# A decoder layer with sparse attention on one NeuronCore: where the rotary embedding's products and sums stand in the attention's queues

## The chip, the core and the metric

The kernel runs on one core of a Trainium2 chip. A core has five engines with a queue each, taken in order: TensorE (PE in the profile, with PEld for its weight loads), VectorE (DVE), ScalarE (ACT), GpSimd (POOL) and SyncE (SP), which here only starts DMAs. The metric is device time in microseconds, the median of several executions. One execution was also recorded by the hardware profiler, and all rows come from it.

## The reference

One layer in float32 over 512 tokens of width 1024, then a final norm:

```
h = rms_norm(x);  proj = h @ w_in          # u, q, kc, vc, ks, vs, kw, vw, g_nsa, g_merge
y_pool = causal pooling mixer of u (windows 2, 4, 8, 16)
y_nsa  = gate0 * softmax(q k_cmp) v_cmp    # 31 compressed blocks of keys
       + gate1 * softmax(q ks) vs          # selected blocks: with 8 blocks and 16 picks, all of them
       + gate2 * softmax(q kw) vw          # sliding window of 512: all causal keys
x += (g_a * (y_pool @ w_proj_pool) + g_b * (y_nsa @ w_proj_nsa)) @ w_out
x += square(relu(rms_norm(x) @ w_ff1)) @ w_ff2
out = rms_norm(x)
```

There are 16 heads of 64 in two groups. q, ks and kw (and the compressed keys) get the rotary embedding, rope: `x * cos + rot(x) * sin`, where rot swaps the two halves of 32 of each head, with a sign.

## The kernel before

Float32 is kept by splitting operands in a high and a low half (fp32r); a product is three matmuls, high by high, high by low, low by high. A weight tile of 1024 columns is loaded to `raw` (L235), copied to a high half on ScalarE (L351) and subtracted to a low half on VectorE or GpSimd (L353).

The first stage (to about 180 us) projects the keys, the values, the first three q and the pooling mixer. The attention stage (about 183 to 388 us) walks over 96 *slots*, 12 for each of the 8 pairs of heads: slots 0 to 3 of a pair are its first half (query blocks 0 and 1, both branches together), slots 4 to 11 its second half, the long ones (blocks 2 and 3, one branch each). After it come the output projection and the MLP (from about 480 us), in a fast matrix product whose sums of weights are made in DRAM by copies (L265, on SP) and accumulating DMAs (L273, on GpSimd), some of them during the attention.

One slot i goes through: scores into a PSUM bank on TensorE (`score_pe`, L1016, three banks); masked negative maximum on VectorE (`smax`, L1038); exponential with its sum on ScalarE (`expo`, L1048); a reciprocal on VectorE (L1058) and the weighting by it and the gate on GpSimd (`weight`, L1061); four slots later the transposition on TensorE (`turn_pe`, L1078, two banks); the high half of the result on ScalarE (`turn_hi`, L1089) and the low half on VectorE (`turn_lo`, L1093), the *PT*; two slots later the product with the values (`pv`, L1112). Once per pair `cmp_scores` does the compressed branch, L952 to L988, whose normaliser times gate, `c` of 128x8, is the small gate product (L973, VectorE), followed by three GpSimd operations (L975, L977, L978); its result opens each accumulation `psO` (L1103), which also needs the sums that empty the bank before (L1121, VectorE).

Between the slots stands *filler*: the projections of q3 to q7 and of the merge gate's second half (`fill2`, L394, 24 matmuls each), advanced so that it is spread over the slots. Each q goes through `rope`: ScalarE evacuates the bank to `rx` (L619), four DMAs on SP write its swapped quarters to `rs` (L622), four products with the cosine and sine tables, half a row each, in place (L631: on VectorE in the first stage, on GpSimd in the attention), two sums on VectorE (L634, L636), and then `q_done` makes Q's high halves on ScalarE (L661, L662) and low halves on VectorE (L664, L666). There is one `rx` and one `rs`, and the next q's projection isn't begun before the rope in hand is done (`scored["rope"]`).

`rope`, `cmp_scores` and others are generators: each `yield` passes on to the other work, and `step_side` steps all that are under way once per slot. In the attention a product of the rope isn't emitted unless the slot before was one of a second half (`slot["long"]`), and it is put behind that slot's weighting (`slot["scaled"]`, through `behind`, which places an instruction after another in issue order). The emission order is not the final one: a scheduler orders each engine's instructions from it, with all dependences kept. q3's rope falls in pair 0, q4's in pair 1, q5's in pair 2, q6's in pair 3 and q7's in pair 5.

Of the kernel before, what the change touches and what calls it, by code (L numbers as in the profile page):

```python
# [13 lines left out]
F32 = mybir.dt.float32  # L14
FR = mybir.dt.float32r
AF = mybir.ActivationFunctionType
ALU = mybir.AluOpType
# [45 lines left out]
def trunk(ctx: ExitStack, tc: tile.TileContext, A, out):  # L63
    nc = tc.nc
    PE, ACT, DVE, POOL = nc.tensor, nc.scalar, nc.vector, nc.gpsimd
    PSUM = bass.MemoryType.PSUM

    def pool(name, **kw):
        return tc.tile_pool(name=name, bufs=1, reuse_waits="tile", **kw)
# [206 lines left out]
    mode = {"pool": False, "first": POOL}  # L276
# [202 lines left out]
    op = e2.enter_context(pool("op"))  # L479
# [8 lines left out]
    GT = ap.tile([128, NT, 48], F32, name="GT")  # L488
# [40 lines left out]
    def behind(made):  # L529
        return tc.issue_after(made.ins)  # L530
# [3 lines left out]
    def sums0(i):  # L534
        junk = p0.tile([128, D], F32, tag="junk", bufs=1, name="junk")
        ACT.activation(junk, xt[i], AF.Square, accum_out=rr[i][:, 0:1])
        r = ACT.activation(rr[i][:, 1:2], rr[i][:, 0:1], AF.Sqrt, bias=eps_t, scale=1.0 / D)
        DVE.reciprocal(rr[i][:, 2:3], rr[i][:, 1:2])
        for h in range(2):
            c = slice(512 * h, 512 * h + 512)  # L540
            v = DVE.scalar_tensor_tensor(xt[i][:, c], xt[i][:, c], rr[i][:, 2:3], psg[h], op0=ALU.mult, op1=ALU.mult)
        return r, v
# [10 lines left out]
    def evac0(i, after=None):  # L553
        sl = slice(128 * i, 128 * i + 128)
        for a in range(2):
            ks = slice(4 * a, 4 * a + 4)
            r = ACT.activation(hT[0][:, ks, sl], trs[i][a], AF.Copy)
            with behind(after) if after else nullcontext():
                v = DVE.tensor_tensor(hT[1][:, ks, sl], trs[i][a], hT[0][:, ks, sl].bitcast(F32), op=ALU.subtract)
        return r, v  # L560
# [9 lines left out]
    r, _ = evac0(1)  # L570
    stir(3)
    with behind(r):
        sums0(2)
        r, v = sums0(3)
# [33 lines left out]

    scored = {"pairs": 0, "rope": 0}
    last_exp = []  # L610
    slot = {"long": False, "scaled": None}

    def rope(ps, scale, done, after=0):

        assert not scored["rope"]
        scored["rope"] = 1
        xr = ap.tile([128, S], F32, tag="rx", bufs=1, name="rx")
        sw = ap.tile([128, S], F32, tag="rs", bufs=1, name="rs")
        ACT.activation(xr, ps, AF.Copy, scale=scale)  # L619
        for b in range(4):  # L620
            a = b ^ 1
            nc.sync.dma_start(sw[32 * b:32 * b + 32, :], xr[32 * a:32 * a + 32, :])  # L622
        yield
        eng = POOL if mode["pool"] else DVE
        hs = [slice(0, S // 2), slice(S // 2, S)]
        for c in hs:
            for t, table in ((xr, cosT), (sw, sinT)):
                while mode["pool"] and not slot["long"]:
                    yield
                with behind(slot["scaled"]) if mode["pool"] else nullcontext():  # L630
                    eng.tensor_tensor(t[:, c], t[:, c], table[:, c], op=ALU.mult)  # L631
                yield
                if c is hs[1] and t is xr:
                    DVE.tensor_tensor(xr[:, hs[0]], xr[:, hs[0]], sw[:, hs[0]], op=ALU.add)  # L634
        yield
        DVE.tensor_tensor(xr[:, hs[1]], xr[:, hs[1]], sw[:, hs[1]], op=ALU.add)  # L636
        while scored["pairs"] < after:
            yield
        for _ in done(xr):
            yield  # L640
        scored["rope"] = 0
# [16 lines left out]
    def q_done(p):  # L658
        def done(q):
            t = ap.tile([128, 2, S], FR, tag="Q", bufs=3, name="Q")  # L660
            ACT.activation(t[0:64, 0, :], q[0:64, :], AF.Copy)  # L661
            ACT.activation(t[64:128, 1, :], q[64:128, :], AF.Copy)  # L662
            yield
            DVE.tensor_tensor(t[64:128, 0, :], q[0:64, :], t[0:64, 0, :].bitcast(F32), op=ALU.subtract)  # L664
            yield
            DVE.tensor_tensor(t[0:64, 1, :], q[64:128, :], t[64:128, 1, :].bitcast(F32), op=ALU.subtract)  # L666
            Q[p] = t
        return done
# [223 lines left out]
    with ExitStack() as c2:  # L892
# [54 lines left out]
        def cmp_scores(p):  # L947
            g = p // 4
            ps = ps2.tile([128, NT, 2, 64], F32, tag="S", bufs=S_BANKS, name="psC")
            for qb in range(NT):  # L950
                for h in range(2):
                    PE.matmul(ps[:, qb, h, :], Q[p][:, h, 128 * qb:128 * qb + 128], KC[g], start=True, stop=True,  # L952
                              skip_group_check=True)
            w = p2.tile([128, NT, 2, 64], F32, tag="cw", bufs=1, name="cw")
            s8 = p2.tile([128, 3, 8], F32, tag="c8", bufs=1, name="c8")
            cm = cst[:, C_CM:C_CM + 128].rearrange("p (q n) -> p q n", q=NT)
            wl = w[:, :, :, 0:32]
            wf = w.rearrange("p q h n -> p (q h) n")[:, :, 0:32]
            DVE.tensor_tensor(wl, ps[:, :, :, 0:32], cm[:, :, None, :].to_broadcast([128, NT, 2, 32]), op=ALU.add)
            sc = ps.rearrange("p q h n -> p (q h) n")[:, :, 0:32]  # L960
            DVE.tensor_tensor(ps[:, :, :, 0:32], ps[:, :, :, 32:64], wl, op=ALU.add)
            yield
            DVE.tensor_reduce(s8[:, 0, :], sc, axis=AX.X, op=ALU.min)
            DVE.tensor_tensor(wf, sc, s8[:, 0, :, None].to_broadcast([128, 8, 32]), op=ALU.subtract)
            yield
            yield
            yield
            ACT.activation(wl, wl, AF.Exp, scale=-1.0)
            yield
            DVE.tensor_reduce(s8[:, 1, :], wf, axis=AX.X, op=ALU.add)  # L970
            DVE.reciprocal(s8[:, 2, :], s8[:, 1, :])
            r = s8[:, 2, :].rearrange("p (q h) -> p q h", q=NT)
            DVE.tensor_tensor(r, r, GT[:, :, 6 * p:6 * p + 6:3], op=ALU.mult)  # L973
            yield
            POOL.tensor_tensor(wl, wl, r[:, :, :, None].to_broadcast([128, NT, 2, 32]), op=ALU.mult)  # L975
            pH, pL = (PC[:, :, e, :].rearrange("p q (h n) -> p q h n", h=2) for e in range(2))
            POOL.tensor_scalar(pH, wl, 1.0, 1.0, op0=ALU.mult, op1=ALU.mult)  # L977
            POOL.tensor_tensor(pL, wl, pH.bitcast(F32), op=ALU.subtract)  # L978
            yield
            yield  # L980
            yield
            yield
            pt = ps2.tile([128, S], F32, tag="T", bufs=T_BANKS, name="psT")
            for qb in range(NT):
                src = PC[:, qb, :, :].rearrange("p e c -> p (e c)")
                PE.transpose(pt[:, 128 * qb:128 * qb + 128].bitcast(FR), src, identR)
            t = p2.tile([128, S], FR, tag="pc", bufs=1, name="pc")
            ACT.activation(t, pt, AF.Copy)  # L988
            PTc[p] = t
# [100 lines left out]

        def turn_lo(i):
            src, dH, dL = turn_views(i)
            DVE.tensor_tensor(dL, src, dH.bitcast(F32), op=ALU.subtract)  # L1093
            live.pop(i)

        def pv(i):
            p, half, br, qb, h = slots[i]
# [37 lines left out]
        for i in range(n + LAG + PLAG):  # L1135
            if i < n:
                p = slots[i][0]
                if i % 12 == 3 and p + 1 < NPAIR:
                    while p + 1 not in Q:
                        fill()  # L1140
                        step_side()
                if i % 12 == CMP_AT and p + 1 < NPAIR:
                    side.append(cmp_scores(p + 1))
            if i + 1 < n:
                score_pe(i + 1)
                scored["pairs"] = (i + 2) // 12
            t = i - LAG
            if 0 <= t < n:
                turn_pe(t)
                turn_hi(t)  # L1150
            if i < n:
                smax(i)
                expo(i)
            if 0 <= i - 1 < n:
                last = weight(i - 1)
                slot.update(long=i > 3 and slots[i - 1][1] == 1, scaled=last)
            if i > 7 and i % 4 == 3 and len(begun) > 1:
                add_sum(last)
            if 0 <= t < n:
                turn_lo(t)  # L1160
            step_side()
            want = done0 + (total - done0) * (i + 1) // (n + LAG + PLAG)
            while fdone[0] < want and fill():
                pass
            if i < 5:
                fill()
            j = t - PLAG
            if 0 <= j < n and j % 2 == 1 and pv(j):
                o_evac(*slots[j][0:2])
# [492 lines left out]
```

## Time and profile before

| what | value |
|---|---|
| median of 3 runs | 811.16 us (810.91 to 811.49) |
| the profiled execution | 812.4 us |
| its span, first to last instruction | 810.6 us |
| mean granted TensorE clock | 0.995 |
| TensorE busy | 786.0 us, 97% |
| VectorE busy | 621.0 us, 77% |
| ScalarE busy | 491.3 us, 61% |
| GpSimd busy | 188.8 us, 23% |

A row of an operation gives the line, the engine, the operation, output and inputs, and a count; after the bar busy time, mean duration, and idle time before it with what ended it. In the chronological rows the first number is the start in us, the second the duration, and brackets hold the idle time of the engine just before and its releaser.

### The profile page before, as it was taken

How to read it: one execution, taken by the hardware profiler on the slowest of the kernel's cores; microseconds unless marked ns; L12 is line 12 of the kernel's file. 1: busy time of each engine (PE TensorE's matmuls, PEld its weight loads, DVE VectorE, ACT ScalarE, POOL GpSimd, SP SyncE). 2: the span in 40 equal slices, each digit the busy share in tenths (PEclk: the TensorE clock that was granted, in tenths of full speed). 3: DMA queues.
4: the chain of work that ended last, by engine and by line, in shares of the span. 5: the costliest groups of instructions: out<-in, count | busy, mean ns of one | idle time of the engine just before them, and what ended most of it. 6: DMA issues, size and time to landing. Idle time of an engine off the chain costs nothing.

```text
span 810.6 us, 14129 instructions
## 1 busy us (share of the span) xinstructions
PE 786.0 (97%) x5163; PEld 708.2 (87%) x5163; DVE 621.0 (77%) x1231; ACT 491.3 (61%) x968; POOL 188.8 (23%) x259
## 2 busy tenths in 40 slices
PE   8999999999799999899999999999999999999996
PEld 6889878888677888788888899999999999999996
DVE  5786744539888888789555579996889688978975
ACT  6666533329777888799534476844674467447833
POOL 4000000028676867666010100111010110000000
PEclk9999999999999999999999999999999999999999
DMA  9464632353587524353975706999998998654522
GB/s 294 139 175 109 178 92 89 107 156 92 98 188 153 104 71 96 77 108 74 310 207 181 184 1 190 324 232 292 255 279 220 288 258 230 192 177 156 181 80 105
DMA packets 128751, 136.65 MB, mean 169 GB/s; under 512 B 5349, under 2 KB 117001, under 8 KB 128522
## 3 DMA queue, kind: packets, MB, share of 16 engines
q1 hardware_dynamic: 107274, 113.98, 43.5%
q0 software_dynamic: 21120, 20.97, 18.1%
q8 instruction: 41, 0.67, 0.3%
q10 hardware_dynamic: 288, 0.79, 0.3%
q14 instruction: 28, 0.23, 0.1%
HBM read 131.01 MB, written 44.04 MB: 216 GB/s over the span
## 4 chain that ended last, share of the span: by engine, by line
PE 74%; DVE 14%; ACT 5%; issue 3%; DMA 2%; POOL 2%; ACTq 0%; DVEq 0%; POOLq 0%
PE psF L394 22%; PE psB L1389 12%; PE psB L394 11%; PE psB L1508 11%; PE psO L1112 3%; PE psT L1078 3%; PE psS L1016 3%; DVE wl L308 2%; PE psV L394 2%; DMA raw<-w_ff 2%; PE psF L451 1%; DVE P L1038 1%; ACT P L1048 1%; DVE PT L1093 1%; PE psC L716 1%
## 5 line engine op out<-in xcount | busy, mean ns | idle before, releaser
L394 PE MATMUL psF<-R,wh 128*128 128x512 f32 x512 | 167.1, 404 | 0.8 <-ACT GB L690 0.6
L306 ACT ACTIVATE wh<-raw 128x1024 fp32r<-128x1024 f32 x70 | 74.0, 1058 | 77.1 <-PE psB L1508 32.0
L351 ACT ACTIVATE wh<-raw 128x512 fp32r<-128x512 f32 (+1 forms) x100 | 60.1, 620 | 94.3 <-PE psF L394 38.2
L273 POOL DMA_DIRECT2D S<-w_ff x40 | 46.1, 1154 | 276.2 <-DMA S<-w_ff 219.5
L394 PEld LDWEIGHTS psF<-R,wh 128*128 128x128 f32 x512 | 92.7, 189 | 19.0 <-ACT GB L690 0.8
L394 PE MATMUL psF<-R,wl 128*128 128x512 f32 x256 | 102.1, 399 | 0.6 <-DVE wl L353 0.6
L308 DVE TENSOR_TENSOR wl<-raw,wh 128x1024 fp32r<-128x1024 f32 x70 | 85.4, 1221 | 20.2 <-ACT wh L306 20.2
L1061 POOL TENSOR_SCALAR P<-P,sm,GT 128x128 f32<-128x128 f32 (+3 forms) x128 | 86.1, 702 | 44.3 <-DVE sm L1058 30.2
L353 DVE TENSOR_TENSOR wl<-raw,wh 128x512 fp32r<-128x512 f32 (+1 forms) x84 | 59.2, 715 | 36.7 <-ACT wh L351 36.2
L1048 ACT ACTIVATE P<-P,sm 128x128 f32<-128x128 f32 (+3 forms) x128 | 71.1, 557 | 14.2 <-DVE sm L1038 10.4
L1038 DVE CUSTOM_DVE_ANT_0 P<-psS,cst 128x128 f32<-128x128 f32 (+3 forms) x128 | 59.7, 484 | 7.8 <-PE psT L1078 6.1
L1389 PE MATMUL psB<-R,wh 128*128 128x256 f32 x352 | 64.1, 282 | 0.0
L1089 ACT ACTIVATE PT<-psT 128x512 fp32r<-128x512 f32 (+2 forms) x96 | 49.2, 519 | 17.1 <-PE psT L1078 16.2
L1078 PE MATMUL psT<-ident,P 128*128 128x128 f32 x320 | 51.4, 275 | 7.7 <-POOL P L1061 4.0
L1093 DVE TENSOR_TENSOR PT<-psT,PT 128x512 fp32r<-128x512 f32 (+2 forms) x96 | 56.5, 595 | 2.9 <-ACT PT L1089 2.0
L394 PEld LDWEIGHTS psF<-R,wl 128*128 128x128 f32 x256 | 48.4, 189 | 11.5 <-DVE wl L353 0.7
L306 ACT ACTIVATE w3h<-raw 128x1024 fp32r<-128x1024 f32 x35 | 37.0, 1056 | 34.9 <-PE psB L1508 16.4
L1078 PEld LDWEIGHTS psT<-ident,P 128*128 128x128 f32 x320 | 39.6, 141 | 18.4 <-POOL P L1061 10.4
L1389 PEld LDWEIGHTS psB<-R,wh 128*128 128x128 f32 x352 | 54.1, 189 | 0.3 <-DVE R L1331 0.2
L1389 PE MATMUL psB<-R,wl 128*128 128x256 f32 x176 | 49.5, 281 | 0.0
L308 DVE TENSOR_TENSOR w3l<-raw,w3h 128x1024 fp32r<-128x1024 f32 x35 | 42.7, 1220 | 8.4 <-ACT w3h L306 8.4
L1112 PE MATMUL psO<-PT,VV 128*128 128x256 f32 x320 | 48.0, 285 | 0.0
(390 smaller groups left out, 2259.8 us busy)
## 6 DMA issues: line engine op xcount, KB each, us to landing
raw<-w_ff SPq DMA_DIRECT2D x55, 512.0 KB, 5.5
S<-w_ff POOLq DMA_DIRECT2D x40, 512.0 KB, 7.4
raw<-S SPq DMA_DIRECT2D x40, 512.0 KB, 4.3
raw<-w_in SPq DMA_DIRECT2D x32, 512.0 KB, 4.1
S<-w_ff SPq DMA_DIRECT2D x30, 512.0 KB, 5.5
S<-S SPq DMA_DIRECT2D x10, 512.0 KB, 6.8
raw<-w_proj_nsa SPq DMA_DIRECT2D x8, 512.0 KB, 4.1
raw<-w_out SPq DMA_DIRECT2D x8, 512.0 KB, 4.3
```

The costliest lines, as they stand in the source:

```text
L306: ACT.activation(h, t, AF.Copy)
L308: DVE.tensor_tensor(l, t, h.bitcast(F32), op=ALU.subtract)
L351: ACT.activation(h[:, sl], t[:, sl], AF.Copy)
L394: PE.matmul(ps, a, b, start=first and j == 0, stop=last and j == n - 1, skip_group_check=True)
L1038: DVE.tensor_tensor_reduce(out=P[:, o:o + n].rearrange("p (a c) -> p a c", c=128), in0=s, in1=m, scale=1.0, scalar=3e38, op0=ALU.add, op1= ...
L1048: last_exp[:] = [ACT.activation(c, c, AF.Exp, bias=sm[:, 0, e:e + 1], scale=-1.0, accum_out=sm[:, 1, e:e + 1])]
L1061: r = POOL.tensor_scalar(P[:, o:o + n], P[:, o:o + n], sm[:, 2, e:e + 1], GT[:, qb, c + e:c + e + 1], op0=ALU.mult, op1=ALU.mult)
L1078: PE.transpose(pt[:, 128 * j:128 * j + 128], P[:, 128 * j:128 * j + 128], ident)
L1093: DVE.tensor_tensor(dL, src, dH.bitcast(F32), op=ALU.subtract)
L1112: PE.matmul(ps[:, qb % 2, :, :], VV[:, k, b, g, :], t[:, j, :, :], start=False, stop=last and j == len(kbs) - 1 and t is tL, skip_group_ch ...
L1389: PE.matmul(out, w[u][:, k, 128 * f:128 * f + 128], XB[x][v][:, k, :], **kw)
L1508: PE.matmul(out, YB[y][u][:, k, 128 * f:128 * f + 128], w[v][:, k, :], **kw)
```

## The change

In the attention (`in_slots`) the rope yields three times more before its first product. The first sum is no longer emitted between the products but after all four, the second a yield later, and each is put behind the low half of the slot's PT (`slot["low"]`, the instruction that `turn_lo` returns). In the first stage the first sum also moves behind the fourth product. `q_done` loses the yield between its two subtractions. In `cmp_scores` the small gate product moves from VectorE to GpSimd, to the far side of the yield. No operation is added or removed.

```diff
@@ rope
         eng = POOL if mode["pool"] else DVE
         hs = [slice(0, S // 2), slice(S // 2, S)]
+        in_slots = mode["pool"]
+        if in_slots:
+            for _ in range(3):
+                yield
+
+        def add(c):
+            with behind(slot["low"]) if in_slots else nullcontext():
+                DVE.tensor_tensor(xr[:, c], xr[:, c], sw[:, c], op=ALU.add)
+
         for c in hs:
             for t, table in ((xr, cosT), (sw, sinT)):
-                while mode["pool"] and not slot["long"]:
+                while in_slots and not slot["long"]:
                     yield
-                with behind(slot["scaled"]) if mode["pool"] else nullcontext():
+                with behind(slot["scaled"]) if in_slots else nullcontext():
                     eng.tensor_tensor(t[:, c], t[:, c], table[:, c], op=ALU.mult)
                 yield
-                if c is hs[1] and t is xr:
-                    DVE.tensor_tensor(xr[:, hs[0]], xr[:, hs[0]], sw[:, hs[0]], op=ALU.add)
-        yield
-        DVE.tensor_tensor(xr[:, hs[1]], xr[:, hs[1]], sw[:, hs[1]], op=ALU.add)
+            if c is hs[0]:
+                continue
+            add(hs[0])
+            yield
+            add(hs[1])
@@ q_done
             DVE.tensor_tensor(t[64:128, 0, :], q[0:64, :], t[0:64, 0, :].bitcast(F32), op=ALU.subtract)
-            yield
             DVE.tensor_tensor(t[0:64, 1, :], q[64:128, :], t[64:128, 1, :].bitcast(F32), op=ALU.subtract)
@@ cmp_scores
-            DVE.tensor_tensor(r, r, GT[:, :, 6 * p:6 * p + 6:3], op=ALU.mult)
-            yield
+            yield
+            POOL.tensor_tensor(r, r, GT[:, :, 6 * p:6 * p + 6:3], op=ALU.mult)
             POOL.tensor_tensor(wl, wl, r[:, :, :, None].to_broadcast([128, NT, 2, 32]), op=ALU.mult)
@@ turn_lo
-            DVE.tensor_tensor(dL, src, dH.bitcast(F32), op=ALU.subtract)
             live.pop(i)
+            return DVE.tensor_tensor(dL, src, dH.bitcast(F32), op=ALU.subtract)
@@ the loop over the slots
             if 0 <= t < n:
-                turn_lo(t)
+                slot["low"] = turn_lo(t)
             step_side()
```

More of the change, by code (lines that the diff above doesn't have):

```diff
@@ L610, in trunk @@
     last_exp = []
-    slot = {"long": False, "scaled": None}
+    slot = {"long": False}
     def rope(ps, scale, done, after=0):
```

## The prediction

> **What bounds the kernel now.** I read the profile's page first, then the busy time by stage, then what TensorE waited for, and last the instructions in order of time around the two longest waits.
>
> ```profile
> span 810.6 us, 14129 instructions
> PE 786.0 (97%) x5163; PEld 708.2 (87%) x5163; DVE 621.0 (77%) x1231; ACT 491.3 (61%) x968; POOL 188.8 (23%) x259
> ```
>
> TensorE (PE) is busy 97% of the span, so a gain can only come out of the 24.6 us in which it is not, or out of a lower clock. By stage (us, then busy time of PE, PEld, DVE, ACT and POOL, granted clock, DMA share, GB/s):
>
> ```profile
> 200.00:250.00 50.00, 44.64 (x277) 37.65 (x276) 41.84 (x131) 36.20 (x98) 36.44 (x51) 1.00 0.68 139
> 300.00:350.00 50.00, 47.04 (x301) 41.46 (x300) 40.52 (x138) 39.11 (x107) 32.99 (x48) 0.97 0.39 80
> 600.00:700.00 100.00, 99.60 (x836) 99.19 (x835) 87.94 (x106) 59.24 (x78) 10.44 (x9) 1.00 0.94 252
> ```
>
> The MLP (third row) has no idle TensorE; the attention has, and the change acts there. What TensorE waited for between 180 and 390 us (total, times, longest):
>
> ```profile
> PE psT L1078 <- POOL P L1061: 4.0, 2, 3.1
> PE psT L1078 <- DVE PT L1093: 2.9, 1, 2.9
> PE psO L1103 <- DVE oT L1121: 1.7, 4, 0.7
> ```
>
> Two single waits of about 3 us stand out. The first, in order of time (start, duration; in brackets the idle time before and its releaser):
>
> ```profile
> 204.20 0.51 SPq L622 DMA_DIRECT2D rs<-rx  x1
> 207.34 0.49 SPq L265 DMA_DIRECT2D S<-S  x1
> 207.88 1.85 SPq L622 DMA_DIRECT2D rs<-rx  x3
> 215.38 0.72 POOL L631 TENSOR_TENSOR rx<-rx,cst 128x256 f32<-128x256 f32 x1 [3.85 <-DMA rs<-rx]
> 216.07 1.26 POOL L353 TENSOR_TENSOR wl<-raw,wh 128x512 fp32r<-128x512 f32 x1
> 217.31 0.66 POOL L1061 TENSOR_SCALAR P<-P,sm,GT 128x384 f32<-128x384 f32 x1
> 218.03 0.55 PE L1078 MATMUL psT<-ident,P 128*128 128x128 f32 x3 [3.08 <-POOL P L1061]
> 218.70 0.43 DVE L634 TENSOR_TENSOR rx<-rx,rs 128x256 f32<-128x256 f32 x1 [3.19 <-POOL rs L631]
> 220.45 2.77 DVE L973 TENSOR_TENSOR c<-c,GT 128x8 f32<-128x8 f32 x1
> 222.29 0.66 PE L1078 MATMUL psT<-ident,P 128*128 128x128 f32 x4 [0.96 <-POOL P L1061]
> 224.12 0.47 PE L1103 MATMUL psO<-pc,VC 128*128 128x256 f32 x2 [0.70 <-DVE oT L1121]
> ```
>
> I call this stall A (q4's rope, slot 17). SyncE (SP) issued one of the four swap DMAs, sat behind the copy S<-S until 207.34, and issued the other three after it. GpSimd's first product then waited 3.85 us for them, with a weight split and slot 17's weighting queued behind it, and the transposition waited for that. VectorE stood in its rope sum, and then 2.77 us in an 8-column product. A cost 3.08 + 0.96 + 0.70 = 4.74 us of TensorE. The second wait, stall B (q7's rope):
>
> ```profile
> 324.96 0.86 ACT L1089 ACTIVATE PT<-psT 128x384 fp32r<-128x384 f32 x2
> 325.84 0.74 POOL L631 TENSOR_TENSOR rs<-rs,cst 128x256 f32<-128x256 f32 x1
> 326.53 1.28 POOL L353 TENSOR_TENSOR wl<-raw,wh 128x512 fp32r<-128x512 f32 x1
> 326.62 1.47 DVE L636 TENSOR_TENSOR rx<-rx,rs 128x256 f32<-128x256 f32 x1 [1.62 <-POOL rs L631]
> 328.01 0.15 DVE L1058 RECIPROCAL sm<-sm 128x1 f32<-128x1 f32 x1
> 328.68 1.01 DVE L1093 TENSOR_TENSOR PT<-psT,PT 128x384 fp32r<-128x384 f32 x2
> 329.37 1.09 PE L1078 MATMUL psT<-ident,P 128*128 128x128 f32 x4 [2.91 <-DVE PT L1093]
> ```
>
> ScalarE had the high halves of slots 64 and 65 ready by 325.82. VectorE's low halves of them (328.68) stood behind the second rope sum, which waited for GpSimd's last product and then ran 1.47 us instead of 0.43. Slot 66's transposition had no free bank before the low half, hence the 2.91 us.
>
> **The change part by part.** *The sums behind the products and each slot's low half.* In the order of the built program, q7's two sums now stand behind the low halves of slots 65 and 66. Nothing of the rope is then ahead of slots 64 and 65 on VectorE, and they can run at about 325.8, which takes the 2.91 us away. What is late next: slot 68's weighting behind that same weight split, which ends at 327.81; TensorE has slot 66's and 67's transpositions, six filler products and a score before it, so I put that at nothing. With the gap its clock goes too:
>
> ```profile
> 326.00:328.00 2.00, 0.47 (x2) 0.03 (x1) 1.38 (x1) 1.01 (x3) 1.80 (x2) 1.00 0.28 43
> 328.00:330.00 2.00, 0.63 (x3) 0.66 (x4) 2.00 (x7) 0.81 (x2) 0.67 (x1) 0.69 0.40 111
> 330.00:332.00 2.00, 2.00 (x8) 1.62 (x7) 1.92 (x8) 1.48 (x3) 0.66 (x1) 0.50 1.04 340
> ```
>
> Lost to it: 0.63 x 0.31 + 2.00 x 0.50 = 1.2 us. So B is worth 2.9 + 1.2 = **4.1 us**; bounds 2.9 (the clock falls elsewhere) and 4.1.
>
> [...]
>
> *Three yields ahead of the products.* For four of the five ropes here GpSimd's first product stands in the same place, since it waits for a slot of the pair's second half anyway. In A it still stands right behind slot 16's weighting and still needs the swap DMAs; but two, not three, now follow the copy on SP (ScalarE's evacuation is earlier, rx being free sooner since q_done lost a yield), one issue or 1.85 / 3 = 0.6 us less, and the weight split has moved ahead of it. Slot 17's transposition can start at about 214.8 + 0.72 + 0.66 = 216.2, which leaves 1.3 of 3.08. The 0.96 I expect to remain at 1.2, since slot 19's weighting has the same GpSimd work ahead; the 0.70 goes, as VectorE no longer stands in L973. New: 30 filler products now stand together behind slot 19's transposition, and the second 17 need weights whose split is behind q4's late sums; an estimate of 1.0 us, from the sum's wait in A. Left 3.5 of 4.74: **1.2 us** gained. Bounds: 4.7, if the DMAs land early, and minus 2, if the weights are 3 us late like the sum.
>
> *q6's rope misses its half.* Its three yields carry it past pair 3's second half: one product behind slot 47, the others behind 52 to 54, the sums and Q some ten slots later. Two waits of TensorE near its old place should go, 0.68 + 0.59 = **1.27 us**:
>
> ```profile
> 281.13 0.47 PE L1103 MATMUL psO<-pc,VC 128*128 128x256 f32 x2 [0.68 <-ACT P L1048]
> 287.42 0.63 PE L1078 MATMUL psT<-ident,P 128*128 128x128 f32 x4 [0.59 <-ACT pc L988]
> ```
>
> Against that, q7's projection waits for that rope, and between slots 53 and 59 TensorE has 4 filler products where it had 18; the 14 follow after slot 59. No work is added, but a hole is made in which TensorE goes at the pace of VectorE. Its rows:
>
> ```profile
> L1016 PE MATMUL psS<-KH,Q x96: 277/392/481, 183.1 to 377.1; 128*128 128x512 f32 x48, 128*128 128x384 f32 x32, 128*128 128x256 f32 x16
> L394 PE MATMUL psF<-R,wh 128*128 128x512 f32 x202 | 69.0, 416 | 0.0
> 230.78 5.39 PE psF L394 x22
> L1038 DVE CUSTOM_DVE_ANT_0 P<-psS,cst 128x128 f32<-128x128 f32 (+3 forms) x128 | 59.7, 484 | 7.8 <-PE psT L1078 6.1 <-POOL P L1061 0.7
> L1093 DVE TENSOR_TENSOR PT<-psT,PT 128x512 fp32r<-128x512 f32 (+2 forms) x96 | 56.5, 595 | 2.9 <-ACT PT L1089 2.0
> L664 DVE TENSOR_TENSOR Q<-rx,Q 64x512 fp32r<-64x512 f32 x5 | 5.2, 1040 | 0.7 <-ACT Q L661 0.6
> ```
>
> A slot takes 194.0 / 96 = 2.02 us. A filler product takes 5.39 / 22 = 0.245; there are 202 with high halves of the weights and half as many with low ones, 303 in all or 74 us, 0.77 a slot. So a slot without filler is 1.25 us, and six with four products 8.5 us. VectorE has between the maxima of slots 53 and 59: 7 maxima (3.4), 7 low halves (4.2), Q's two subtractions (2.1), the two sums (0.9), six reciprocals (0.9) and some ten like the 0.43 us sum (4.2): 15.6 us. The hole is worth between nothing (three score banks and transpositions four slots behind let TensorE run ahead by up to three slots, some 6 us) and 15.6 - 8.5 = 7.1. I take **minus 1.5**, nearer the low end because VectorE had caught up before it.
>
> *The small gate product on GpSimd.*
>
> ```profile
> L973 DVE TENSOR_TENSOR c<-c,GT x8: 150/207/2765, 177.5 to 352.1; 128x8 f32<-128x8 f32 x8
> L781 POOL TENSOR_SCALAR VC<-VC x4: 292/294/830, 124.2 to 128.3; 32x128 fp32r<-32x128 f32 x4
> L975 POOL TENSOR_TENSOR cw<-cw,c x8: 617/618/1019, 177.8 to 352.4; 128x256 f32<-128x256 f32 x8
> ```
>
> VectorE loses eight of 0.21 us and the one of 2.77 (counted in A). GpSimd gains eight of between 0.29 and 0.62 us; I take 0.3, the smaller tile being nearest: 2.4 us in 170, hidden in its idle third (33 of 50 us busy above). Without that cover it is 5 us at most.
>
> *The rest*: the sums and Q's subtractions swap places in the first stage too, and there VectorE takes them without GpSimd; the MLP isn't touched. Both at nothing, TensorE being full.
>
> Sum: 4.1 + 1.2 + 1.3 - 1.5 = 5.1 us. The profiled execution took 812.4 (span 810.6 and 1.8 around it), so 807.3; it was 1.2 above the median of 811.16, and against that the forecast is **806.1**.
>
> **The rivals.**
> *The hole decides (slower).* If TensorE has no lead when it reaches slot 53, it loses the 7.1 us, and with a drop of the clock as in B 1.2 more: 811.16 - 6.6 + 8.3 = 812.9. It decides from 6.6 us on. For it: VectorE is busy 40.5 of 50 us there, and the rope's work now falls into the hole. Against it: the filler-poor slots 13 to 23 of today lost 4.74 us only with a DMA wait among them.
> *VectorE's sums collide with GpSimd (slower).* L636 ran 1.47 us beside a GpSimd split, 1.04 over the free sum. Ten sums so, all on the path, make 10.4 us: 816.5. Against it: the sum at 218.70 took 0.43, and what follows the sums now is not needed at once. [...]
> *The gain is swallowed (no change).* The MLP's loads hold the DMA engines at 0.94 busy; if they set its pace once the attention ends earlier, the end stays at 811. Against it: TensorE is busy 99.6 of 100 us there.
> *Better.* The DMAs land before GpSimd asks, and TensorE runs through the hole: 811.16 - 4.1 - 4.7 - 1.3 = 801.
>
> **How the numbers follow.** Forecast 0.60 (own range 803.5 to 809.5), better 0.07, swallowed 0.08, the hole 0.20, collisions 0.05. A measurement here can tell about 0.2%, 1.6 us: faster 0.67, same 0.08, slower 0.25. The range 802.5 to 812.5 leaves out most of the collisions, the lower end of "better" and the worst of the hole.
>
> **What would show it.** Right: no idle TensorE ahead of the transposition of slot 66, and a granted clock of 1.00 from 320 to 340; VectorE never 1 us in front of a rope sum, but for q4's second; A's first gap near 1.3 us; eight GpSimd products of 128x8 at 0.3; the idle TensorE of the two attention rows above down from 5.4 and 3.0 us to about 4 and 0. Wrong: idle gaps of some us between slots 53 and 59, a clock drop there, a fill that waits for weights after slot 24, or A's gap unchanged at 3 us.

## The result and the profile after

The changed kernel takes 803.32 us (median of 6 runs, 801.03 to 804.33) against 811.33 (median of 6, 810.91 to 812.07): a ratio of 0.9894, 95% interval 0.9878 to 0.991, so it is faster by 1.1%. The forecast was 806.1 with a range of 802.5 to 812.5. The profiled execution of the changed kernel is the fastest of its six, 801.03 us; beside it the profiled 812.4 of before makes 11.4 us, 3.4 more than the medians do. Sums over the two profiles are therefore too large by about that much.

The page of the changed kernel, its span and busy times:

```profile
span 799.3 us, 14120 instructions
PE 783.4 (98%) x5163; PEld 707.4 (89%) x5163; DVE 615.8 (77%) x1223; ACT 490.6 (61%) x968; POOL 189.4 (24%) x267
```

The place of the gain is seen by cutting each span at the end of its attention, 390 us before and 379 us after (columns as in the prediction: the stretch, its length, busy time of PE, PEld, DVE, ACT and POOL, granted clock, DMA share, GB/s). The stages of the kernel before:

```profile
200.00:390.00 190.00, 178.51 (x1134) 154.70 (x1133) 159.80 (x513) 154.42 (x409) 128.01 (x174) 0.99 0.53 112
390.00:810.00 420.00, 411.90 (x3032) 390.07 (x3030) 333.67 (x438) 232.32 (x349) 30.63 (x26) 1.00 0.73 206
```

and of the changed one, with three stretches inside its attention:

```profile
200.00:379.00 179.00, 176.37 (x1135) 154.03 (x1134) 154.84 (x507) 153.56 (x408) 127.91 (x181) 1.00 0.56 119
379.00:799.00 420.00, 411.25 (x3030) 389.74 (x3028) 333.27 (x437) 231.97 (x349) 30.62 (x26) 1.00 0.73 206
...
200.00:250.00 50.00, 49.48 (x320) 43.20 (x319) 43.40 (x141) 41.03 (x110) 42.39 (x60) 1.00 0.74 148
300.00:350.00 50.00, 49.19 (x322) 43.36 (x321) 42.43 (x149) 41.82 (x116) 37.11 (x56) 1.00 0.52 110
...
320.00:340.00 20.00, 19.62 (x131) 17.52 (x130) 17.90 (x63) 16.63 (x47) 11.86 (x18) 1.00 0.37 80
```

What follows the attention takes 420 us in both: nothing was gained there, and nothing given back. The attention lost 11 us, of which 8.9 are idle TensorE (190 - 178.51 = 11.5 before, 179 - 176.37 = 2.6 after). The two stretches that held the stalls went from 5.4 and 3.0 us of idle TensorE to 0.5 and 0.8. All that TensorE still waits for between 180 and 390 us (total, times, longest):

```profile
PE psS L1025 <- DVE sm L1047: 1.1, 2, 0.7
PE psT L995 <- DVE PT L1103: 1.0, 3, 0.4
PE psO L1112 <- DVE oT L1130: 0.2, 1, 0.2
PE psT L1087 <- POOL P L1070: 0.2, 1, 0.2
```

The waits of 3.1 and 2.9 us are both gone. Stall A's place, in order of time (start, duration; in brackets the idle time before and its releaser):

```profile
202.16 1.14 SPq L622 DMA_DIRECT2D rs<-rx  x2
206.64 0.49 SPq L265 DMA_DIRECT2D S<-S  x1
207.18 1.22 SPq L622 DMA_DIRECT2D rs<-rx  x2
...
208.37 1.71 POOL L353 TENSOR_TENSOR wl<-raw,wh 128x512 fp32r<-128x512 f32 x1
212.03 0.74 POOL L640 TENSOR_TENSOR rx<-rx,cst 128x256 f32<-128x256 f32 x1 [0.28 <-DVE sm L1067]
216.90 1.76 DVE L633 TENSOR_TENSOR rx<-rx,rs 128x256 f32<-128x256 f32 x1
217.51 0.66 PE L1087 MATMUL psT<-ident,P 128*128 128x128 f32 x4 [0.20 <-POOL P L1070]
```

Two swap DMAs, not one, are out ahead of the copy S<-S; the last is started by 208.40, where it was 209.73. GpSimd's first product starts 3.35 us earlier than before (212.03 against 215.38) and waits for no DMA in this execution. The weight split L353, which stood behind that product at 216.07, now fills the time before it. And the sum at 216.90 runs 1.76 us beside GpSimd's back-to-back work, but no transposition is behind it. Stall B's place:

```profile
316.98 0.85 ACT L1098 ACTIVATE PT<-psT 128x384 fp32r<-128x384 f32 x2
317.88 1.02 DVE L1103 TENSOR_TENSOR PT<-psT,PT 128x384 fp32r<-128x384 f32 x2
318.58 0.63 PE L1087 MATMUL psT<-ident,P 128*128 128x128 f32 x4
318.81 0.45 DVE L633 TENSOR_TENSOR rx<-rx,rs 128x256 f32<-128x256 f32 x1
318.93 1.48 POOL L353 TENSOR_TENSOR wl<-raw,wh 128x512 fp32r<-128x512 f32 x1
```

The two low halves follow ScalarE's high halves at once, the transposition has its bank, and the sum (0.45 us, started as soon as VectorE is there) comes after them. The granted clock stays at 1.00 from 320 to 340.

### The profile page after: what moved, and what is told of

Its sections match the earlier page's. It is cut to its first block, busy times and chain, and to the rows that moved or that the text cites. A ratio compares the mean times of both kernels' runs of the same rounds, so it can differ in the third digit from the quotient of the medians.

```text
span 799.3 us, 14120 instructions
## 1 busy us (share of the span) xinstructions
PE 783.4 (98%) x5163; PEld 707.4 (89%) x5163; DVE 615.8 (77%) x1223; ACT 490.6 (61%) x968; POOL 189.4 (24%) x267
## 4 chain that ended last, share of the span: by engine, by line
PE 77%; DVE 13%; ACT 4%; issue 2%; DMA 2%; POOL 1%; SPq 0%; DVEq 0%; ACTq 0%; POOLq 0%
PE psF L394 23%; PE psB L1398 15%; PE psB L394 12%; PE psB L1517 12%; PE psO L1121 3%; PE psS L1025 3%; PE psT L1087 3%; PE psV L394 2%; DVE wl L308 2%; PE psF L451 1%; DVE P L1047 1%; DVE PT L1103 1%; PE psC L725 1%; DMA S<-w_ff 1%; PE psC L961 1%
## 5 line engine op out<-in xcount | busy, mean ns | idle before, releaser
L353 DVE TENSOR_TENSOR wl<-raw,wh 128x512 fp32r<-128x512 f32 (+1 forms) x84 | 58.5, 704 | 35.1 <-ACT wh L351 34.6
```

## The experiments

None of the twelve kernels leaves out any of the work. The ratio is of the mean times of all runs, so it can differ by some 0.1% from that of the medians in the text. *Lead* is the start of a slot's score in the profile of before, minus its start in the run's profile, in us: how far the run is ahead there. Slot 12 opens pair 1 (q4's rope, stall A), and by slot 27 its filler is behind; 48 to 64 is the stretch of q6's moved rope; stall B lies between 70 and 72; 95 is the last slot. The gains of pair 1 and of B are differences of two columns.

```
run                                 ratio to before [95%]     lead at slot 12   27    48    64    72    95
changed kernel                      0.9894 [0.9878, 0.991]             0.7   6.5   6.5   7.7  11.9  11.4
e1  sums only                       0.9972 [0.9959, 0.9986]            1.2  -0.9  -0.9   0.5   4.6   3.2
e2  three yields only               0.9987 [0.9971, 1.0003]            0.2   0.1   0.1   0.1   0.0   0.1
e3  gate product only               1.0028 [1.0008, 1.0048]           -0.4  -1.3  -1.5  -1.7  -0.8  -2.0
e4  q_done's yield only             1.0    [0.9985, 1.0016]           -0.3  -0.8  -2.1  -2.3  -1.0  -1.1
e5  three yields and q_done         0.9923 [0.9905, 0.9941]            1.3   7.3   6.9   8.2   8.1   7.0
u1  changed, but sums as before     0.9961 [0.9946, 0.9975]           -0.2   3.5   3.1   4.6   4.9   4.2
u2  changed, without three yields   0.9924 [0.9899, 0.9949]            1.0  -1.1   0.1   1.1   5.2   4.8
u3  changed, gate on VectorE        0.9911 [0.9885, 0.9937]            1.1   5.6   5.7   6.4  10.6   9.4
u4  changed, q_done as before       0.9941 [0.9918, 0.9963]           -0.1   1.5   1.4   1.2   5.4   4.7
x1  before, swaps from ScalarE      1.0054 [1.0038, 1.007]            -4.0  -0.1  -0.2  -0.5  -3.0  -4.4
x2  changed, swaps from ScalarE     0.9969 [0.9957, 0.9982]           -0.9   4.7   1.3   2.5   6.8   5.7
x3  changed, q6's rope not moved    0.9894 [0.9873, 0.9915]            1.2   5.1   5.1   6.1  10.3   9.5
```

### Each part alone

e1 takes over the hunk of the sums (with `turn_lo`'s return value):

```diff
+        def add(c):
+            with behind(slot["low"]) if mode["pool"] else nullcontext():
+                DVE.tensor_tensor(xr[:, c], xr[:, c], sw[:, c], op=ALU.add)
...
+            if c is hs[0]:
+                continue
+            add(hs[0])
+            yield
+            add(hs[1])
```

> The kernel before with only the sums moved behind all four products and each slot's PT. Theory one (the sums standing on VectorE ahead of other slots' low halves cost stall B, the swap DMAs behind the copy cost stall A, each by itself): B goes with its clock drop, A stays, 807 us (-3.5 to -4.5). Theory two (the gain is one thing, the start of pair 1 and what follows from it): within 1 us of before, 810.5. TensorE's wait for the transposition behind GpSimd's weighting near 217 us stays at 2 to 3 us by both.

810.1 us (before 812.64), ratio 0.9972. B is gone: the lead grows by 4.1 us between slots 64 and 72, and the stretch from 300 us, and then A in order of time, read

```profile
300.00:350.00 50.00, 48.53 (x317) 42.66 (x315) 43.08 (x149) 40.54 (x112) 35.02 (x51) 1.00 0.42 84
```

```profile
215.21 0.73 POOL L635 TENSOR_TENSOR rx<-rx,cst 128x256 f32<-128x256 f32 x1 [3.71 <-DMA rs<-rx]
217.86 0.55 PE L1083 MATMUL psT<-ident,P 128*128 128x128 f32 x3 [2.91 <-POOL P L1066]
```

Idle TensorE fell from 3.0 to 1.5 us there and the clock stayed at 1.00, while A stands nearly as before. So the sums are the cure of B and none of A; by the ratio they are worth 2.3 us, less than B, and in this profile pair 1 fell back by 2.1. Of that, 1.7 us are clock: it halved behind A's gap, where it had stayed at 1.00 before.

```profile
218.00:222.00 4.00, 4.00 (x19) 3.66 (x19) 2.44 (x3) 2.73 (x7) 4.00 (x6) 0.57 0.22 12
```

e2 takes over only the three yields:

```diff
+        if mode["pool"]:
+            for _ in range(3):
+                yield
```

> The kernel before with only the three yields ahead of the rope's products in the attention. In the built program this moves nothing but q6's rope, from pair 3 to slots 47 to 54. Theory one: q6's place gives 1.7 us, the hole between slots 53 and 59 costs 0.3, 809.9 us. Theory three (the distance between the DMAs and the products is what the gain came from): 805 us and no DMA wait ahead of q4's first product.

811.65 us, ratio 0.9987: no difference that this measurement can tell. q4's first product waits as long as before:

```profile
207.43 1.85 SPq L622 DMA_DIRECT2D rs<-rx  x3
215.30 0.72 POOL L634 TENSOR_TENSOR rx<-rx,cst 128x256 f32<-128x256 f32 x1 [4.27 <-DMA rs<-rx]
```

e3 moves only the small gate product:

```diff
-            DVE.tensor_tensor(r, r, GT[:, :, 6 * p:6 * p + 6:3], op=ALU.mult)
-            yield
+            yield
+            POOL.tensor_tensor(r, r, GT[:, :, 6 * p:6 * p + 6:3], op=ALU.mult)
```

> The kernel before with only the small gate product on GpSimd. Theory one: VectorE loses 2.6 us of contention in stall A, of which TensorE sees the 0.7 us wait ahead of the compressed branch's product, 810.5 us; eight GpSimd products of 0.2 to 0.3 us. Theory four (the 2.77 us on VectorE was what drew out pair 1): 808 us or less.

814.07 us, ratio 1.0028: alone, this part costs. It took 2.77 us of VectorE out of A's stretch and TensorE gained nothing by it. Of the rows there, one shows where some of it went back (the second rope sum ran 0.47 us before):

```profile
223.00 0.57 POOL L974 TENSOR_TENSOR c<-c,GT 128x8 f32<-128x8 f32 x1
223.45 1.62 DVE L636 TENSOR_TENSOR rx<-rx,rs 128x256 f32<-128x256 f32 x1 [0.29 <-POOL rs L631]
```

e4 takes out only the yield between Q's two subtractions:

```diff
             DVE.tensor_tensor(t[64:128, 0, :], q[0:64, :], t[0:64, 0, :].bitcast(F32), op=ALU.subtract)
-            yield
             DVE.tensor_tensor(t[0:64, 1, :], q[64:128, :], t[64:128, 1, :].bitcast(F32), op=ALU.subtract)
```

> The kernel before with only the yield between Q's two subtractions removed. Two of q4's four swap DMAs then go ahead of the copy, but the first product moves up from behind slot 16's weighting to behind slot 14's. Theory one: the DMAs land near 212, GpSimd asks near 209 and stands some 3 us with slots 15 and 16 behind it, so A is about as long as before or longer, 811 to 814 us. Theory five (the yield alone cured A): 805.5 us.

812.61 us, ratio 1.0. This does start the swap DMAs earlier, two of them ahead of the copy. But the rope then also reaches its first product earlier, the scheduler puts that behind slot 14's weighting, not slot 16's, and GpSimd waits with two more slots' weightings behind it. (The trace names no releaser for that wait; the last packet of the swaps began at 214.67, as long ahead of the product as in the other runs that waited, 0.7 us.)

```profile
215.36 0.72 POOL L631 TENSOR_TENSOR rx<-rx,cst 128x256 f32<-128x256 f32 x1 [5.62 <-issue]
216.68 1.19 PE L1077 MATMUL psT<-ident,P 128*128 128x128 f32 x4 [4.59 <-POOL P L1060]
```

The four parts alone add to -0.13%; together they make -1.06%.

### One part undone

u1 is the changed kernel with the sums as before:

```diff
-            if c is hs[0]:
-                continue
-            add(hs[0])
-            yield
-            add(hs[1])
+                if c is hs[1] and t is xr:
+                    DVE.tensor_tensor(xr[:, hs[0]], xr[:, hs[0]], sw[:, hs[0]], op=ALU.add)
+        yield
+        DVE.tensor_tensor(xr[:, hs[1]], xr[:, hs[1]], sw[:, hs[1]], op=ALU.add)
```

> The changed kernel with the sums put back where they were, the rest kept. Theory one: B comes back with 3.5 to 4.1 us, A stays gone: 807.2 us. Theory two (one thing, pair 1): 803.5 us.

808.93 us (before 811.91), ratio 0.9961. B is back in its place, with every other part still in:

```profile
PE psT L1080 <- DVE PT L1095: 3.2, 1, 3.2
```

u2 is the changed kernel without the three yields:

```diff
-        if in_slots:
-            for _ in range(3):
-                yield
```

> The changed kernel without the three yields. q4's first product moves up behind slot 14's weighting, and q6's rope goes back into pair 3. Theory one: GpSimd waits some 3 us for the swap DMAs in pair 1 and 4 to 6 us of A come back, 808 us. Rival (the yields do nothing but move q6's rope): 804.5 us.

805.74 us, ratio 0.9924. In its profile A is worse than before the change, by the same mechanism as in e4 (GpSimd's first product at 214.45 after 5.90 us of idleness, a TensorE gap of 4.8 us, pair 1 2.1 us behind); B gives its 4.1 us. The time lies between the two that were expected: by the ratios the yields are worth less than these profiles say, 2.4 us beside the other three parts, and the two intervals overlap.

u3 has the gate product on VectorE again, u4 the yield in `q_done`:

```diff
-            yield
-            POOL.tensor_tensor(r, r, GT[:, :, 6 * p:6 * p + 6:3], op=ALU.mult)
+            DVE.tensor_tensor(r, r, GT[:, :, 6 * p:6 * p + 6:3], op=ALU.mult)
+            yield
```

> The changed kernel with the small gate product back on VectorE. Theory one: within 1 us of the changed kernel, 803.3 to 804.3. Theory four (the gate product's contention drew out pair 1): 806 us.

804.67 us, ratio 0.9911; its interval overlaps that of the changed kernel.

```diff
             DVE.tensor_tensor(t[64:128, 0, :], q[0:64, :], t[0:64, 0, :].bitcast(F32), op=ALU.subtract)
+            yield
             DVE.tensor_tensor(t[0:64, 1, :], q[64:128, :], t[64:128, 1, :].bitcast(F32), op=ALU.subtract)
```

> The changed kernel with the yield between Q's subtractions put back. Only one swap DMA of q4 goes ahead of the copy then. Theory one: the DMA wait of about 3.9 us ahead of q4's first product comes back, and 3 to 5 us with it, 807 us. Theory three (the three yields are enough by themselves): 803.5 us.

808.21 us, ratio 0.9941. Pair 1 gains 1.6 us where the changed kernel gains 5.8: the swap DMAs are late again (three behind the copy, the last started by 209.86), and the first product waits 3.08 us for them. So q_done's yield, which the prediction mentioned in half a sentence, carries much of A.

### The two that make A

e5 is the kernel before with e2's and e4's edits together, sums and gate product untouched.

```diff
+        if mode["pool"]:
+            for _ in range(3):
+                yield
...
-            yield
             DVE.tensor_tensor(t[0:64, 1, :], q[64:128, :], t[64:128, 1, :].bitcast(F32), op=ALU.subtract)
```

> The kernel before with two of the four edits: the three yields ahead of a rope's products and the yield that q_done loses; the sums and the gate product stay. Alone these two moved pair 1 (lead at the score of slot 27) by 0.1 and -0.8 us; with the gate product added they moved it by 3.5, with all four by 6.5. Theory 'pair' (the two together are what lets q4's first product go without a DMA wait, the early evacuation by the one and the place behind slot 16 by the other): the wait for the swap DMAs ahead of that product falls from 3.85 to under 2.5 us, the lead at slot 27 is 2.5 to 4, stall B stays at 2.9, and the time falls by 2.5 to 4, from 811.3 to 807.3-808.8. Rival 'three of four' (it needs the gate product off VectorE's queue, too, or GpSimd's order that came with it): the lead at slot 27 is under 1.5 us and the time 810 to 812.

805.95 us (before 812.95), ratio 0.9923: more than either theory allowed. Neither edit alone moved the time by more than 1.0 us; together they take 7.0 by the medians and 6.3 by the ratio. Its chronological rows at A and B, and then the row of B's stretch:

```profile
201.11 1.14 SPq L622 DMA_DIRECT2D rs<-rx  x2
206.28 1.22 SPq L622 DMA_DIRECT2D rs<-rx  x2
207.25 1.77 POOL L353 TENSOR_TENSOR wl<-raw,wh 128x512 fp32r<-128x512 f32 x1
211.65 0.74 POOL L634 TENSOR_TENSOR rx<-rx,cst 128x256 f32<-128x256 f32 x1 [0.96 <-DVE PT L1095]
...
318.42 1.47 DVE L639 TENSOR_TENSOR rx<-rx,rs 128x256 f32<-128x256 f32 x1 [1.61 <-POOL rs L634]
321.18 1.09 PE L1080 MATMUL psT<-ident,P 128*128 128x128 f32 x4 [2.90 <-DVE PT L1095]
```

```profile
300.00:350.00 50.00, 46.79 (x289) 41.27 (x287) 39.72 (x133) 37.81 (x101) 33.28 (x49) 0.93 0.46 101
```

A is gone but for 0.5 us (pair 1 gains 6.0 us), B is untouched at 2.90 us, with its slow clock behind it. The one edit starts the DMAs earlier; the other keeps the first product behind slot 16's weighting and lets the weight split into the time before it. With the first alone the product is early and waits in front of slot 15; with the second alone the DMAs are late. This also splits the result: 0.9923 for these two and 0.9972 for the sums alone make -1.05%, against -1.06% for the whole change. Each of these has an interval of some 0.15%; within it, the gate product isn't needed.

### Who makes the swap DMAs late

x1 and x2 start the attention's swap DMAs from ScalarE, where SP's copy can't hold them; x1 from the kernel before, x2 from the changed one.

```diff
-            nc.sync.dma_start(sw[32 * b:32 * b + 32, :], xr[32 * a:32 * a + 32, :])
+            (ACT if mode["pool"] else nc.sync).dma_start(sw[32 * b:32 * b + 32, :], xr[32 * a:32 * a + 32, :])
```

> The kernel before, with one edit: the four swap DMAs of a rope in the attention are started from ScalarE's queue, where the evacuation that they need also is, and no longer from SP's, where the copy S<-S can stand ahead of them. Theory 'queue' (the late landing of q4's swap DMAs comes from their place behind the copy on SP, and it is what stall A costs): q4's first product on GpSimd waits under 0.5 us for a DMA where it waited 3.85, the wait of 3.08 us ahead of slot 17's transposition goes, pair 1 gains 3 to 4.7 us by slot 27, and the time falls from 812 to about 808.5. Rival 'transfers' (they are late because the copy and the accumulating DMA occupy the DMA engines at the same time): the DMAs start at about 204 us and still land 4 us or more later, the product waits 2 us or more, and the time is 811.5 to 812.5. Rival 'the product's place' (the DMA wait is only one of several things that hold slot 17): the DMA wait goes, but the lead at slot 27 is under 1.5 us, and the time 810.5 to 812.

> The changed kernel with the same edit, the swap DMAs of the ropes in the attention from ScalarE's queue. Theory 'queue': in the changed kernel q4's first product waits no more for a DMA (0.28 us for slot 16's reciprocal), so nothing is left to gain at pair 1; the time stays at 803.3, within 0.8. Rival 'transfers': the same time, too, since the DMAs already land early enough. Rival 'ScalarE': each of the twenty starts takes time on ScalarE's queue ahead of exponentials that TensorE needs; the time rises to 804.5 or more.

x1 took 815.7 us, x2 809.25 (before 811.11): ratios 1.0054 and 0.9969, so the edit cost 4.6 and 5.9 us, and for x2 the rival "ScalarE" is borne out. The rows of x1 at q4's rope:

```profile
207.24 0.58 ACT L619 ACTIVATE rx<-psF 128x512 f32<-128x512 f32 x1
207.85 0.51 ACTq L622 DMA_DIRECT2D rs<-rx  x1
208.41 1.89 ACTq L622 DMA_DIRECT2D rs<-rx  x3
210.34 0.40 ACT L1048 ACTIVATE P<-P,sm 128x128 f32<-128x128 f32 x1 [2.14 <-DVE sm L1038]
```

Four starts take ScalarE's queue for some 2.4 us, and an exponential stands behind them (2.14 us of idleness, which the trace puts down to an earlier releaser); x2 shows the same at 206.41, with 2.18 us. The starts that nobody waits for on SP delay the softmax on ScalarE. The DMA wait at q4's first product did go in x1, and pair 1 gained 4.0 us, as "queue" had it; but the rope itself also began 3.7 us later (its evacuation at 207.24 against 203.57, the lead being at -4.0 by slot 12), so this doesn't show "queue" right. The landing speaks for "transfers" as well: with the copy far behind them (212.32) and only the accumulating DMA under way, the four still took a median of 4.3 us from start to landing. As for the 5.6 us of before, from the last start (done at 209.73) to the product at 215.38, the trace's DMA packets, the pieces in which a transfer is moved, tell more. Those of the copy end at 211.29. From then on the DMA engines are full of the accumulating DMA (q0, started by GpSimd), and the last packets of the swaps (q1, started by SP) come thinly among its own until 214.70 (between 211.6 and 215 us: packets, MB, share of the 16 DMA engines):

```profile
q0 software_dynamic: 454, 0.45, 93.0%
q1 hardware_dynamic: 49, 0.07, 6.5%
```

So the copy is under way in the first 1.6 us of that wait, and the accumulating DMA takes most of the rest: "queue" is a part of it, "transfers" the larger one. That an early start alone doesn't settle the landing is seen in u2: SP starts its last two swaps at 207.19, as in the changed kernel (207.18), GpSimd starts the accumulating DMA 0.2 us earlier (207.42 against 207.62), and the swaps' last packet begins at 213.72 instead of 211.02.

### q6's place

x3 is the changed kernel with the three yields left out for q6's rope only, so that its products stand behind slots 45 to 47 again.

```diff
-            for _ in range(3):
+            for _ in range(0 if after == 4 else 3):
```

> The changed kernel, with the three yields left out for q6's rope alone, so that it catches pair 3's second half as before the change (products behind slots 45 to 47, not 47 and 52 to 54). Theory 'the later place pays a little' (predicted: 1.27 us for two waits that go, less 1.5 for the hole; the profile showed a lead that grows by 1.2 us from slot 48 to slot 64): the lead over the kernel before no longer grows between slots 48 and 64, and the time rises by 1.2 to 804.5. Rival 'the hole costs more than the place gives': TensorE has 18 filler products again between slots 53 and 59, and the time falls to 802.5 or less. Rival 'nothing': 803.3 within 0.5, the two cancelling as predicted.

803.27 us, ratio 0.9894: the same as the changed kernel, though with an interval of 1.7 us to either side the 1.2 of the first theory can't be told from nothing. Between slots 48 and 64 its lead grows by 1.0 us, with q6's rope moved by 1.2. Its waits of TensorE between 250 and 310 us:

```profile
PE psS L1025 <- DVE sm L1047: 1.1, 2, 0.7
PE psT L1087 <- DVE PT L1103: 0.5, 1, 0.5
```

Neither of the two waits that I wanted to remove by the move is there, without the move. And e2, which moves q6's rope and gains nothing at A or B, has a lead of 0.1 us at slot 48 as at slot 64. And in the changed kernel, slots 53 to 59 take 8.1 us (283.5 to 291.6) with a full TensorE:

```profile
283.00:292.00 9.00, 9.00 (x64) 8.09 (x63) 8.60 (x26) 7.63 (x20) 6.06 (x9) 1.00 0.37 117
```

x3 says one more thing. Up to q6's rope its instructions stand in the changed kernel's order, yet pair 1 gained 3.9 us in its profile and 5.8 in the other. Where the changed kernel's first product of q4 had an idle time of 0.28 us before it, and slot 19's transposition one of 0.20, x3 has

```profile
213.44 0.75 POOL L640 TENSOR_TENSOR rx<-rx,cst 128x256 f32<-128x256 f32 x1 [2.19 <-DVE PT L1103]
218.91 0.66 PE L1087 MATMUL psT<-ident,P 128*128 128x128 f32 x4 [1.27 <-POOL P L1070]
```

The trace has no landing of the fourth swap DMA and names a low half in its place. But the swaps' last packet begins at 212.79, 0.65 us ahead of the product, and before the change at 214.70, 0.68 us ahead, so this is most likely the wait for the swaps again. u1 and u3 have it too (2.45 and 1.52 us), and TensorE loses 1.3 to 2.0 us to it in these three. With the wait added, pair 1 comes to between 6.0 and 6.2 us in all four profiles, so what tells u1, u3, x3 and the changed kernel apart there (3.7, 4.5, 3.9 and 5.8 us) goes with the landing of the swaps and is no evidence on the edits. The changed kernel's profile, the fastest of its six runs, is the one of the four in which the swaps were in time; how often they are is not known.

## Why the prediction was right, and where it was not

*What bounds the kernel*: right. All of the gain is idle TensorE and clock in the attention, and the 420 us behind it are as they were.

*Stall B, 4.1 us*: right, in size and cause. The lead grows by 4.1 us from slot 64 to 72 in e1 and by 4.2 in the changed kernel, B stands at 2.90 in e5 and 3.2 in u1, where the sums are as before, and the clock went with it. The weighting of slot 68, which I put at nothing, cost at most the 0.6 us by which the lead falls back to slot 76 in the changed kernel (11.85 to 11.23). That the clock's 1.2 us belong to B holds for the profile of before; in e4 the same gap left the clock alone (1.00 from 300 to 350 us).

Before the change the clock was halved at B for 3.41 us, from 328.77 to 332.18. I cut the attention into stretches of that length, counted from this drop, and in e5 from its own at 320.24. The stretch ahead of B's drop before the change, the one in which A's gap ended, where the clock stayed, and the one ahead of the drop in e5:

```profile
325.36:328.77 3.41, 1.10 (x7) 0.62 (x5) 2.15 (x5) 1.65 (x5) 2.95 (x4) 1.00 0.40 63
216.13:219.54 3.41, 1.51 (x12) 1.39 (x12) 0.84 (x3) 0.93 (x3) 3.41 (x4) 1.00 0.02 2
316.83:320.24 3.41, 1.45 (x10) 0.97 (x8) 1.82 (x3) 1.99 (x6) 2.94 (x5) 1.00 0.54 88
```

Of the 64 such stretches from 180 to 395 us before the change, the first of these rows has the least busy TensorE and the second the next. A gap of 2.9 us cost clock in some executions and not in another: at B it left the granted clock of 300 to 350 us at 0.97 in e2, at 1.00 in e4 and at 0.93 in e5. So the length of a gap alone does not tell whether the clock is lost; what does was not shown.

*Stall A, 1.2 us*: the mechanism was named and the size was wrong; this is the term of the sum that was mis-sized. Pair 1 gained 5.8 us by the profile and 6.0 in e5 (the bound was 4.7), and still 3.7 to 4.5 in u1, x3 and u3, where a wait at the first product remained. I left 3.5 of 4.74 us standing, from three estimates. The first gap, left at 1.3: I moved the product by what one DMA's issue takes, 0.6 us, and kept the landing of before. But the product had stood 5.6 us behind the last start, and now stands 3.6 behind it (208.40 to 212.03), with the start itself 1.3 us earlier; the gap became 0 here and in u3, and 0.59 and 0.85 us in x3 and u1. Slot 19's wait, at 1.2: it was 0.20 here, but 1.27 in x3 and in u3 and 1.19 in u1, so this estimate holds where the swaps land late. The late weights of the filler, at 1.0: no such wait appeared in any of them; one of 0.58 us that stood there before the change (at 230.78 us), and that the 4.74 leave out, went instead. The first and third were priced as if q4's rope would end about as late as before; once its first product moved up by 3.35 us, all that hung on it moved up too. I also named the wrong edit: the heading was the three yields, and alone they do nothing that can be measured; they need the yield that `q_done` lost.

*q6's rope, +1.27 and -1.5*: the net of about nothing is what x3 measured, within its 1.7 us, but by the traces neither term was there. The two waits go without the move, and the hole cost no idle TensorE; the lead that falls from 9.9 to 7.9 us between slots 58 and 60 is the 14 filler products being made up, as the prediction says. The hole's price was the lower of the two bounds, nothing.

*The gate product, nothing*: its duration was 0.206 us where I took 0.3 from the nearest row:

```profile
L983 POOL TENSOR_TENSOR c<-c,GT x8: 200/206/842, 177.1 to 340.8; 128x8 f32<-128x8 f32 x8
L633 DVE TENSOR_TENSOR rx<-rx,rs x20: 408/421/1983, 35.7 to 321.0; 128x256 f32<-128x256 f32 x20
```

In the changed kernel it costs nothing that can be measured. On its own it cost 0.28%, which I had not allowed for; u1 against e5, which differ by it alone, says the same (0.9961 against 0.9923). With the sums behind the low halves (u3) that cost is gone. Why the two hang together isn't settled; e3's sum of 1.62 us behind the moved product is a trace of it, not a proof.

*The rivals.* The hole did not decide. The sums did run longer beside some of GpSimd's work (second row above: 0.42 us at the median, 1.98 at most, at 249.26 us beside the weight split L353, which ran 1.77 us from 249.18), but off the path, which is what the price of 10.4 us had left out: only what is queued behind a long sum pays, and now it is nothing that TensorE needs at once. Nothing was swallowed by the MLP. The rival "better", at 801, describes what happened in the profiled execution: DMAs ahead of GpSimd, TensorE through the hole. x3, with a GpSimd that waits for them again, has a profiled time of 804.51. The median lies between that rival and the forecast, 2.3 us above the one and 2.8 below the other; the profiled execution is at 801.03.

So the direction, the place and B were right, and the forecast of 806.1 was 2.8 us too slow, because of A, which gained 2.5 us more than forecast even in the profile where it gained least (u1): the time lies in the range, and just below the 803.5 at which the likeliest case's own range ended.

## What to carry to other kernels

A wait of an engine on a DMA has two ends: how early the transfer starts, and how late the engine asks. Moving one end alone did nothing that could be measured (ratios of 0.9987 and 1.0 here), both together did all of it (0.9923); so price edits that touch the two ends of a wait as a pair, and see what other work the scheduler can then put into the wait. The landing varies as well: with the same order of instructions the wait was 0.28 us in one profile and 2.19 in another. It went with what else the DMA engines carried: before the change the accumulating DMA's packets held 93.0% of them from 211.6 to 215 us, and the swaps' 6.5%. When a stall is released, move everything that hung on it by the same time before pricing what is late next. And a queue that seems idle enough for a DMA start must be judged by what stands behind it: the starts for five ropes, some 2.4 us each, were free on SP and cost 4.6 and 5.9 us of the time on ScalarE.

## What the runs showed of the hardware

- Four DMA starts held ScalarE's queue: 0.51 us for the first and 1.89 for the other three, about as long as on SP (0.51 and 1.85), with 2.14 us of idle ScalarE behind them.
- A 64 KB swap DMA landed 2.0 to 2.2 us after its start at the median of a run, and at most 4.7 us (changed kernel) to 6.6 us (u4), with DMAs of 512 KB under way, an accumulating one among them; in x1 the four of q4's rope, with no copy ahead of them, took a median of 4.3 us.
- Before the change the TensorE clock was at 0.50 for 3.41 us at B's gap of 2.91 us, and at 1.00 all through A's of 3.08. In e5 a gap of 2.90 us at B left 0.50 from 322 to 326 us; in e4 one of 2.9 left 1.00 from 300 to 350.
- GpSimd took a median of 0.206 us for 128x8 elements with two inputs, the same as VectorE's (0.207), so the size of that product gave no reason to prefer either. The longest of each ran beside the other engine's work: 2.77 us on VectorE (before, at 220.45), 0.84 on GpSimd (changed kernel, at 218.34).
